# High and low part of a 256-token tile as one 512-column matmul operand, in a two-block fp32 network on one Trainium2 core

## The chip, the cores and the metric

One core of a Trainium2 chip runs the whole program. The time is device microseconds of one execution. The engines are TensorE (PE in the profile, its weight loads PEld), VectorE (DVE), ScalarE (ACT), GpSimd (POOL) and SyncE (SP), which issues the DMAs.

## The reference, cut to what matters

A batch of one, 256 tokens, width 1024, all in float32. A first block of two layers, then a second block of two layers in which a second stream (ctx, also 256 tokens) goes along. Every layer is made of feed-forwards and mixers between residuals; nearly all of the work is `activation @ weight`.

```
# first block, each of two layers
x = x + 0.5 * swiglu_ffn(rms_norm(x, g1), w_in, w_out)     # 1024 -> 2 x 2816 -> 1024
rx, rgate, q, k, v, f, ga, gb = split(rms_norm(x, g2) @ w_in)
ya = (rg_lru(causal_dwconv(rx)) * gelu(rgate)) @ w_rnn_out
yb = forgetting_attention(q, k, v, f) @ w_attn_out         # 8 heads of 128, q and k normed per head
x = x + (sigmoid(ga) * ya + sigmoid(gb) * yb) @ w_o
x = x + 0.5 * swiglu_ffn(rms_norm(x, g3), ...)
x = x + sigmoid(rms_norm(x, g4) @ w_gate + b) * (p @ w_proj)
# second block: layer 0 has a convolution module, layer 1 windowed attention with context keys
x   = x   + 0.5 * gt1 * swiglu(modulate(x, ...));   ctx = ctx + 0.5 * cg1 * swiglu(modulate(ctx, ...))
x   = x   + gt2 * (conv or attention of x);         ctx = ctx + cg2 * conv of ctx      # layer 0
x   = x   + 0.5 * gt3 * swiglu(modulate(x, ...));   ctx likewise in layer 0
return rmsnorm(x, final_g)
```

## The kernel before, in words

Activations stand feature-major: 128 features on the partitions, 256 tokens (or both streams, 512) in the free dimension, so a linear layer takes a [128, 128] weight tile as the stationary operand and moves 256 token columns past it. To keep float32 accuracy with the faster float32r matmul, every weight and every activation is split in two parts, high and low, and `mm3` (lines 293 to 297) adds three products in PSUM: high weight by high activation, high by low, low by high.

`Chunk` (lines 271 to 289, called `load`) brings up to sixteen weight tiles by one DMA into `wraw` (two buffers) and splits them in pieces of 1024 columns: ScalarE's cast gives `whi` (line 281), VectorE's subtraction `wlo` (line 282), five buffers of each. The high and low activations lie in separate `big` buffers.

PSUM has eight banks of [128, 512] floats. The pool `pm` has four one-bank buffers with the tag `mm` for the linear layers, `pst` three for small things, `pad` one. `gemm_pair` makes two output tiles side by side in one bank, 16 weight tiles, 48 matmuls. What reads PSUM afterwards is the operation itself: the multiplication with the norm (L420, L652, L663, L719), the residual (`stt`, L370), a Silu (L889), and so on.

First block (`ffn1st`, `mix`, `ple`): only x exists; the norm's factor per token is applied at the eviction, so that matmuls needn't wait for it. `mix` computes q, k and v token-major, with the activation as the stationary side and 256 weight columns moved at a time (`gemm_tok`), norms each head of q and k (squares on ScalarE, L578; powers on GpSimd; scaling on VectorE, L586), and transposes it back on TensorE (L590). Between these, `lru_front` runs the recurrent branch on VectorE and ScalarE.

Second block: `Feed.ins` and `Feed.outs` are a feed-forward, `Conformer` the convolution module, `attend` the attention. `modnorm` makes the split, normed input tile by tile; here the norm comes before the matmul. `pair_s` works on one stream (256 columns), with two chunks at a time where a stage starts, `pair_j` on both (512 columns). Where both streams run together the matmuls have 512 columns already.

`Background` runs the depthwise convolution of the context, a chain of VectorE operations, between the groups of the first block's second layer: each group hands out an estimate of free VectorE time. `filler` runs the modulation's matmuls (L748) in the same manner. The instructions of each engine stand in a fixed order, made when the program is built: the earliest in the program goes first among those that a simulated timeline finds ready.

Of the kernel before, what the change touches and what calls it, by code (L numbers as in the profile page):

```python
# [17 lines left out]
P = 128  # L18
D = 1024
KT = 8  # L20
# [114 lines left out]
def layout(inputs):  # L135
# [35 lines left out]
    for l in range(2):  # L171
# [9 lines left out]
        out[f"qkv{l}"] = _lay_cols(w[:, 2048:5120], 256)  # L181
# [31 lines left out]
def tile_body(ctx, tc, I, out, stop=None, dbg=None):  # L213
# [8 lines left out]
    pm = ctx.enter_context(tc.tile_pool(name="pm", bufs=4, space=PSUM))  # L222
# [75 lines left out]

    def after(ins):
# [3 lines left out]
    def ps(tag="mm"):  # L303
        pool = {"mm": pm, "st": pst, "ad": pad}[tag]
        return pool.tile([P, 512], F32, tag=tag, name=nm("ps" + tag))
# [20 lines left out]
    class Sq:  # L326
        """running sum of squares of one stream's eight feature tiles"""
# [17 lines left out]
    def rs_cols(sq, inv, eps):  # L345
        """[128 tokens, 2] = (inv * column sums + eps) ** -0.5"""
# [13 lines left out]
    def bcast(r):  # L360
        """[128, 256] with r[token] on every partition: in PSUM and copied"""
# [14 lines left out]
    # =====================================================================  # L376
    # first block
    # =====================================================================
    class Pre:
        """gain * x split in two, tile by tile as x is finished, with the sum of squares"""  # L380

        def __init__(self, gain):
            self.gain = gain
            self.h = None

        def add(self, n):
            if self.h is None:
                self.h = bigt([P, KT, S], F32R)
                self.l = bigt([P, KT, S], F32R)
                self.sq = Sq()  # L390
            x = X[:, n, 0:S]
            g = vc(self.gain, n)
            A.activation(self.h[:, n, :], x, AF.Copy, scale=g)
            stt(self.l[:, n, :], x, g, self.h[:, n, :], ALU.mult, ALU.subtract)
            self.sq.add(x)
# [9 lines left out]
    def gemm_pair(W, hh, hl):  # L405
        """two output tiles [128, 256] of a 2048-element chunk, in one bank"""
        b = ps()
        ks = [(j, k) for j in range(2) for k in range(KT - 1)] + [(j, KT - 1) for j in range(2)]
        for j, k in ks:
            mm3(b[:, j * S : (j + 1) * S], *W(j * KT + k), hh[:, k, :], hl[:, k, :], j == 0 and k == 0, j == 1 and k == KT - 1)  # L410
        return b

    def ffn1st(pre, fi, fo, after, hook, first=None):
        pre.done()
        ah = [bigt([P, 8, S], F32R) for _ in range(3)]
        al = [bigt([P, 8, S], F32R) for _ in range(3)]
        for f in range(FT):
            b = gemm_pair(first if first and f == 0 else load(I[fi][f]), pre.h, pre.l)
            t = tmp(512)
            V.tensor_tensor(out=v2(t), in0=v2(b), in1=pre.Rb, op=ALU.mult)  # L420
# [4 lines left out]
            split(ah[f // 8][:, f % 8, :], al[f // 8][:, f % 8, :], a)  # L425
            hook("in", f)
        for n in range(KT):
            b = ps()
            for r in range(2):
                W = load(I[fo][n, :, r * 11 * P : (r + 1) * 11 * P], 11 * P)  # L430
                for j in range(11):
                    f = 11 * r + j
                    mm3(b[:, 0:S], *W(j), ah[f // 8][:, f % 8, :], al[f // 8][:, f % 8, :], f == 0, f == FT - 1)
            x = X[:, n, 0:S]
            stt(x, b[:, 0:S], 0.5, x, ALU.mult, ALU.add)
# [3 lines left out]
    def softplus_table():  # L439
        """2 * softplus(-lam), both layers: [128, 16]"""  # L440
# [23 lines left out]
    def atanh2(o, w, z, h):  # L464
        """o = 2 atanh(w) for 0 <= w <= 1/3 (series to w**15)"""
# [6 lines left out]
    def mix(l, pre, after):  # L472
        pre.done()
        hh, hl, R, Rb, r = pre.h, pre.l, pre.R, pre.Rb, pre.r
        # r2e = eps * (mean(x^2) + eps) per token, for the head norms on unscaled q, k
# [15 lines left out]
        for k in range(KT):  # L491
            mm3(pf[:8, 0:S], fh[:, k * 8 : k * 8 + 8], fl[:, k * 8 : k * 8 + 8], hh[:, k, :], hl[:, k, :], k == 0, k == KT - 1)
# [10 lines left out]
        # minus log sigmoid, then its running sum = -dcum  # L503
# [23 lines left out]
        def lru_front(n):  # L527
            """xb <- -(1 + tanh) x d, th <- tanh(-log a / 2), at <- a, with d = 1 / (1 + th)"""
# [12 lines left out]
            # d from exp, then one Newton step: -d = ((1 + th) d0 - 2) d0  # L541
# [13 lines left out]
        for c in range(4):  # L555
            b = gemm_pair(load(I[f"rx{l}"][c]), hh, hl)
            for j in range(2):
# [825 lines left out]
```

## Time and profile before

| what | us |
|---|---|
| median of three runs | 3210.55 |
| lowest and highest run | 3207.67, 3215.64 |
| span of the profiled execution | 3207.8 |
| VectorE busy in that span | 1939.8 |
| ScalarE busy in that span | 1468.9 |

The profile lists no time of the profiled execution but its span, from the first to the last instruction; it lies within 0.1% of the median. In the profile a matmul's duration is modelled and includes its way through the array: neighbours overlap, so that the price of a matmul in a stream is the distance from one start to the next. Durations on VectorE overlap a little in the same way.

### The profile page before, as it was taken

What the parts mean: (1) busy time and instruction counts of PE and PEld (TensorE: products, weight loads), DVE (VectorE), ACT (ScalarE), POOL (GpSimd) and SP (SyncE); (2) the same over time, 40 slices, a digit from 0 to 9 for tenths busy, and PEclk for the clock granted to TensorE, in tenths of its full rate; (3) what the DMA queues carried; (4) which work ended last, traced back from release to release, by engine and by line L of the source; (5) the groups of instructions that cost most, each with busy time, mean ns of one, the idle gap of its engine ahead of it and who ended that gap; (6) DMA issues with size and microseconds to landing.
All of it is one profiled execution on the core that took longest, in us unless ns stands there. A gap on an engine that the chain in (4) does not pass through costs nothing.

```text
span 3207.8 us, 55462 instructions
## 1 busy us (share of the span) xinstructions
PE 3138.7 (98%) x23080; PEld 2916.9 (91%) x23080; DVE 1939.8 (60%) x3139; ACT 1468.9 (46%) x2421; POOL 341.5 (11%) x410
## 2 busy tenths in 40 slices
PE   9999999999999999999999999999999999999998
PEld 8899899999999999899999998878888888895898
DVE  6557666556558998668767557954333433356554
ACT  4446654445445446545555446643222322246443
POOL 1010102011010010001011025410002000110101
PEclk9999999999999999999999999989999999999999
DMA  7664346764454554345554554775222223230354
GB/s 284 266 231 164 127 163 238 272 221 167 172 183 171 177 188 166 129 160 188 178 175 159 173 169 168 279 285 188 92 87 97 98 88 110 77 112 34 132 177 139
DMA packets 84252, 536.02 MB, mean 167 GB/s; under 512 B 10016, under 2 KB 13088, under 8 KB 32416
## 3 DMA queue, kind: packets, MB, share of 16 engines
q1 hardware_dynamic: 84000, 532.48, 46.9%
q8 instruction: 180, 2.95, 0.4%
q14 instruction: 72, 0.59, 0.0%
HBM read 531.39 MB, written 1.05 MB: 166 GB/s over the span
## 4 chain that ended last, share of the span: by engine, by line
PE 92%; DVE 3%; ACT 1%; POOL 1%; issue 1%; DMA 1%; POOLq 0%; DVEq 0%; SPq 0%; ACTq 0%
PE psmm L294 28%; PE psmm L295 28%; PE psmm L296 28%; PE psad L748 2%; DVE wlo L282 1%; DVE big L370 1%; PE psad L1133 1%; PE psst L1125 1%; PE psst L350 1%; POOL tmp L342 1%; ACT whi L281 1%; DVE tmp L370 1%; PE psst L296 0%; PE psst L294 0%; PE psst L295 0%
## 5 line engine op out<-in xcount | busy, mean ns | idle before, releaser
L294 PE MATMUL psmm<-big,whi 128*128 128x256 f32 (+1 forms) x6546 | 1955.3, 300 | 14.8 <-ACT big L841 10.9
L295 PE MATMUL psmm<-big,whi 128*128 128x256 f32 (+1 forms) x6546 | 1955.6, 299 | 5.0 <-DVE big L370 5.0
L296 PE MATMUL psmm<-big,wlo 128*128 128x256 f32 (+1 forms) x6546 | 1952.6, 299 | 3.1 <-DVE wlo L282 3.1
L281 ACT CAST whi<-wraw 128x1024 fp32r<-128x1024 f32 (+2 forms) x940 | 904.6, 973 | 1320.4 <-PE psmm L295 941.8
L282 DVE TENSOR_TENSOR wlo<-wraw,whi 128x1024 fp32r<-128x1024 f32 (+2 forms) x940 | 1067.2, 1144 | 689.1 <-ACT whi L281 677.9
L294 PEld LDWEIGHTS psmm<-big,whi 128*128 128x128 f32 x6546 | 1260.6, 193 | 88.4 <-issue 19.8
L295 PEld LDWEIGHTS psmm<-big,whi 128*128 128x128 f32 x6546 | 1262.5, 193 | 46.7 <-issue 7.1
L296 PEld LDWEIGHTS psmm<-big,wlo 128*128 128x128 f32 x6546 | 1261.7, 193 | 44.4 <-issue 5.5
L335 POOL TENSOR_TENSOR tmp<-X 128x256 f32<-128x256 f32 x20 | 15.7, 792 | 1670.5 <-DVE X L370 1620.1
L370 DVE SCALAR_TENSOR_TENSOR big<-U,vec,big 128x256 f32<-128x256 f32 x392 | 188.9, 496 | 4.0 <-ACT big L977 0.5
L890 DVE TENSOR_TENSOR tmp<-tmp,psmm 128x256 f32<-128x256 f32 (+1 forms) x120 | 58.9, 491 | 122.8 <-PE psmm L296 118.7
L373 ACT CAST big<-tmp 128x256 fp32r<-128x256 f32 (+1 forms) x210 | 92.5, 441 | 82.8 <-DVE tmp L424 65.1
L420 DVE TENSOR_TENSOR tmp<-psmm,tmp 128x512 f32<-128x512 f32 x88 | 60.7, 690 | 106.3 <-PE psmm L296 105.5
L296 PE MATMUL psmm<-whi,big 128*128 128x256 f32 x416 | 118.3, 284 | 2.0 <-DVE big L370 2.0
L341 POOL TENSOR_TENSOR tmp<-X 128x256 f32<-128x256 f32 x100 | 83.9, 848 | 329.6 <-DVE X L370 272.5
L294 PE MATMUL psmm<-whi,big 128*128 128x256 f32 x416 | 118.8, 286 | 0.1
L295 PE MATMUL psmm<-wlo,big 128*128 128x256 f32 x416 | 118.1, 284 | 0.0
L374 DVE TENSOR_TENSOR big<-tmp,big 128x256 fp32r<-128x256 f32 (+1 forms) x210 | 97.7, 467 | 20.0 <-ACT big L373 19.4
L342 POOL TENSOR_TENSOR tmp<-tmp,tmp 128x256 f32<-128x256 f32 x100 | 102.6, 1030 | 5.3
L370 DVE SCALAR_TENSOR_TENSOR X<-psmm,mods,X 128x256 f32<-128x256 f32 x96 | 43.5, 480 | 74.7 <-PE psmm L296 72.9
L296 PEld LDWEIGHTS psmm<-whi,big 128*128 128x128 f32 x416 | 79.7, 192 | 2.4 <-DVE big L370 2.2
L295 PEld LDWEIGHTS psmm<-wlo,big 128*128 128x128 f32 x416 | 79.8, 192 | 0.1
(271 smaller groups left out, 2012.1 us busy)
## 6 DMA issues: line engine op xcount, KB each, us to landing
big<-ada SPq DMA_DIRECT2D x72, 1024.0 KB, 9.6
wraw<-fi_c SPq DMA_DIRECT2D x66, 1024.0 KB, 4.9
wraw<-fi_d SPq DMA_DIRECT2D x52, 1024.0 KB, 4.9
wraw<-fi_b SPq DMA_DIRECT2D x44, 1024.0 KB, 4.9
wraw<-fi_a SPq DMA_DIRECT2D x43, 1024.0 KB, 4.9
wraw<-fo_c SPq DMA_DIRECT2D x48, 704.0 KB, 4.0
wraw<-qkv SPq DMA_DIRECT2D x24, 1024.0 KB, 4.9
wraw<-pw SPq DMA_DIRECT2D x24, 1024.0 KB, 4.9
```

Source lines behind the costliest of these rows:

```text
L281: A.copy(hi[:, :e], raw[:, o : o + e])
L282: V.tensor_sub(lo[:, :e], raw[:, o : o + e], hi[:, :e])
L294: T.matmul(o, wh, xh, start=start, stop=False)
L295: T.matmul(o, wh, xl, start=False, stop=False)
L296: newest[1] = T.matmul(o, wl, xh, start=False, stop=stop).ins
L341: G.tensor_tensor(out=q, in0=src, in1=src, op=ALU.mult)
L342: G.tensor_tensor(out=self.acc, in0=self.acc, in1=q, op=ALU.add)
L370: V.scalar_tensor_tensor(o, a, s, b, op0, op1)
L373: A.copy(hi, src)
L374: V.tensor_sub(lo, src, hi)
L420: V.tensor_tensor(out=v2(t), in0=v2(b), in1=pre.Rb, op=ALU.mult)
L748: T.matmul(p_[32 * q : 32 * q + 32, :], cs[:, 4 * h + q, 16 - 2 * b : 48 - 2 * b], raw[:, q * 512 : (q + 1) * 512], start=b == 0 and h == ...
```

## The change

The high and low part of an activation tile now lie next to each other in one buffer, `Split`, as [128, tiles, 2, 256]. `mm2` moves both halves past the high weight tile in one matmul of 512 columns, which fill one whole PSUM bank, and then the high half past the low weight tile in one of 256 columns. The sum of the bank's two halves is made when it is read: `add2` copies one half by ScalarE and adds the other by VectorE, into a buffer of its own; `residual` adds the two halves to X one after the other. Two output tiles need two banks, so `pm` becomes two buffers of two banks. `gemm_tok` moves 512 weight columns at a time in place of 256. Where both streams already give 512 columns, in `pp` of `ple`, in `keys_values`, and in the last chunk of the queries, `mm3` stays.

```diff
-    pm = ctx.enter_context(tc.tile_pool(name="pm", bufs=4, space=PSUM))
+    pm = ctx.enter_context(tc.tile_pool(name="pm", bufs=2, space=PSUM))
+    def mm2(o, wh, wl, x, start, stop):
+        T.matmul(o, wh, x, start=start, stop=False)
+        newest[1] = T.matmul(o[:, 0], wl, x[:, 0], start=False, stop=stop).ins
+        return newest[1]
+    class Split:
+        def __init__(self, nt, w=S):
+            self.per = 1024 // w
+            self.t = [bigt([P, self.per, 2, w], F32R) for _ in range(-(-nt // self.per))]
+        def __call__(self, n, c=slice(None)):
+            return self.t[n // self.per][:, n % self.per, :, c]
+    def banks():
+        return pm.tile([P, 2, 512], F32, tag="mm", name=nm("psmm"))
+    def halves(b):
+        return b.rearrange("p a (h s) -> p a h s", h=2)
+    def add2(b):
+        t, u = tmp(512), tmp(512)
+        A.copy(v2(t), halves(b)[:, :, 1])
+        V.tensor_tensor(out=v2(u), in0=halves(b)[:, :, 0], in1=v2(t), op=ALU.add)
+        return u
+    def residual(x, b, j, scale):
+        for h in range(2):
+            stt(x, halves(b)[:, j, h], scale, x, ALU.mult, ALU.add)
...
-    def gemm_pair(W, hh, hl):
-        b = ps()
+    def gemm_pair(W, x):
+        b = banks()
...
-            mm3(b[:, j * S : (j + 1) * S], *W(j * KT + k), hh[:, k, :], hl[:, k, :], j == 0 and k == 0, j == 1 and k == KT - 1)
+            mm2(halves(b)[:, j], *W(j * KT + k), x(k), k == 0, k == KT - 1)
+    def scaled(b, Rb):
+        u = add2(b)
+        V.tensor_tensor(out=v2(u), in0=v2(u), in1=Rb, op=ALU.mult)
+        return u
...
-            t = tmp(512)
-            V.tensor_tensor(out=v2(t), in0=v2(b), in1=pre.Rb, op=ALU.mult)
+            t = scaled(b, pre.Rb)
...
-            stt(x, b[:, 0:S], 0.5, x, ALU.mult, ALU.add)
+            residual(X[:, n, 0:S], b, 0, 0.5)
...
-        def gemm_tok(W):
-            b = ps()
+        def gemm_tok(c):
+            b = banks()
+            Ws = [load(I[f"qkv{l}"][c, h]) for h in range(2)]
+            for k in range(KT):
+                for m in range(2):
+                    tok = slice(m * P, (m + 1) * P)
+                    w = Ws[k // 4](k % 4, 512)
+                    T.matmul(b[:, m], px.h(k, tok), w[0], start=k == 0, stop=False)
+                    T.matmul(b[:, m], px.h(k, tok), w[1], start=False, stop=False)
+                    T.matmul(b[:, m], px.l(k, tok), w[0], start=False, stop=k == KT - 1)
+            return b
...
-    def pair_s(Ws, H, s, tag="mm"):
-        bs = [ps(tag) for _ in Ws]
+    def pair_s(Ws, H, s):
+        bs = [banks() for _ in Ws]
...
-            mm3(bs[i][:, j * S : (j + 1) * S], *Ws[i](j * KT + k), H.h(k, col(s)), H.l(k, col(s)), k == 0 and j == 0, k == KT - 1 and j == 1)
+            mm2(halves(bs[i])[:, j], *Ws[i](j * KT + k), H(k, col(s)), k == 0, k == KT - 1)
...
-                            use(f + q, col(s), b[:, 0:S], b[:, S:512])
+                            t = add2(b)
+                            use(f + q, col(s), t[:, 0:S], t[:, S:512])
```

## Rows read from the trace of the kernel before

**Rows 1.** The page: span, busy time by engine, chain that ended last by engine.
```profile
span 3207.8 us, 55462 instructions
...
PE 3138.7 (98%) x23080; PEld 2916.9 (91%) x23080; DVE 1939.8 (60%) x3139; ACT 1468.9 (46%) x2421; POOL 341.5 (11%) x410
...
PE 92%; DVE 3%; ACT 1%; POOL 1%; issue 1%; DMA 1%; POOLq 0%; DVEq 0%; SPq 0%; ACTq 0%
```

**Rows 2.** PE's groups by shape: xcount | busy us, mean ns | idle before.
```profile
L295 PE MATMUL psmm<-big,whi 128*128 128x256 f32 x5700 | 1626.1, 286 | 5.0 <-DVE big L370 5.0
...
L295 PE MATMUL psmm<-big,whi 128*128 128x512 f32 x846 | 329.5, 390 | 0.0
...
L294 PE MATMUL psmm<-whi,big 128*128 128x256 f32 x416 | 118.8, 286 | 0.1
```

**Rows 3.** PE's timeline, 256 columns: start, us, instruction; 45 matmuls apart.
```profile
101.26 0.28 PE L296 MATMUL psmm<-big,wlo 128*128 128x256 f32 x1
...
106.65 0.28 PE L296 MATMUL psmm<-big,wlo 128*128 128x256 f32 x1
```

**Rows 4.** PE's timeline, 512 columns, 14 matmuls apart.
```profile
2299.69 0.39 PE L294 MATMUL psmm<-big,whi 128*128 128x512 f32 x1
...
2302.86 0.39 PE L296 MATMUL psmm<-big,wlo 128*128 128x512 f32 x1
```

**Rows 5.** Windows: stretch, us, busy PE PEld DVE ACT POOL (x), PEclk, DMA, GB/s.
```profile
490.00:510.00 20.00, 18.89 (x159) 18.69 (x158) 18.96 (x24) 12.12 (x18) 12.95 (x12) 1.00 0.49 163
...
955.00:1111.00 156.00, 153.73 (x1270) 153.64 (x1270) 141.24 (x253) 84.36 (x119) 2.01 (x7) 0.99 0.50 172
1111.00:1186.00 75.00, 75.00 (x628) 75.00 (x627) 66.19 (x114) 33.79 (x50) 12.51 (x20) 1.00 0.61 204
...
1213.00:1301.00 88.00, 84.18 (x675) 82.53 (x674) 70.96 (x148) 64.68 (x156) 8.40 (x7) 1.00 0.42 145
...
1460.00:1536.00 76.00, 76.00 (x636) 76.00 (x635) 61.54 (x98) 42.03 (x56) 1.54 (x4) 1.00 0.53 187
...
2000.00:2100.00 100.00, 97.68 (x789) 85.17 (x788) 84.84 (x161) 61.51 (x124) 39.83 (x57) 0.98 0.72 282
...
3006.00:3130.00 124.00, 124.00 (x1020) 124.00 (x1019) 66.25 (x89) 57.78 (x86) 0.00 (x0) 0.98 0.50 171
```

**Rows 6.** VectorE's groups by shape, columns as in rows 2.
```profile
L282 DVE TENSOR_TENSOR wlo<-wraw,whi 128x1024 fp32r<-128x1024 f32 x804 | 988.6, 1238 | 540.7 <-ACT whi L281 529.8 <-PE psmm L295 3.0 <-PE psst L364 2.1
...
L420 DVE TENSOR_TENSOR tmp<-psmm,tmp 128x512 f32<-128x512 f32 x88 | 60.7, 690 | 106.3 <-PE psmm L296 105.5 <-ACT tmp L366 0.5
...
L370 DVE SCALAR_TENSOR_TENSOR X<-psmm,X 128x256 f32<-128x256 f32 x48 | 19.4, 418 | 15.7 <-PE psmm L296 15.1
```

**Rows 7.** ScalarE's groups by shape.
```profile
L281 ACT CAST whi<-wraw 128x1024 fp32r<-128x1024 f32 x804 | 833.8, 1048 | 1076.8 <-PE psmm L295 698.4 <-issue 133.7 <-PE psmm L296 41.1
...
L1126 ACT COPY big<-psst 128x512 f32<-128x512 f32 x32 | 18.1, 594 | 16.7 <-PE psst L1125 16.6
```

**Rows 8.** VectorE's timeline beside the background: [idle before <-releaser].
```profile
1052.28 0.69 DVE L420 TENSOR_TENSOR tmp<-psmm,tmp 128x512 f32<-128x512 f32 x1 [0.81 <-PE psmm L296]
...
1058.04 0.69 DVE L420 TENSOR_TENSOR tmp<-psmm,tmp 128x512 f32<-128x512 f32 x1 [0.95 <-PE psmm L296]
1058.64 0.48 DVE L370 SCALAR_TENSOR_TENSOR big<-U,vec,big 128x256 f32<-128x256 f32 x1
```

**Rows 9.** VectorE's timeline at 107 us, and where the context's first feed-forward starts.
```profile
106.97 0.69 DVE L420 TENSOR_TENSOR tmp<-psmm,tmp 128x512 f32<-128x512 f32 x1 [2.18 <-PE psmm L296]
...
768.27 2.36 DVE L282 TENSOR_TENSOR wlo<-wraw,whi 128x1024 fp32r<-128x1024 f32 x2 [4.16 <-ACT whi L281]
770.55 0.41 DVE L890 TENSOR_TENSOR tmp<-tmp,psmm 128x256 f32<-128x256 f32 x1
```

**Rows 10.** PE's waits: who <- for whom: us in total, times, longest us.
```profile
PE psmm L294 <- ACT big L841: 10.9, 4, 4.2
...
PE psst L590 <- DVE tmp L586: 8.9, 6, 2.7
```

More of the change, by code (lines that the diff above doesn't have):

```diff
@@ L432, in ffn1st @@
                     f = 11 * r + j
-                    mm3(b[:, 0:S], *W(j), ah[f // 8][:, f % 8, :], al[f // 8][:, f % 8, :], f == 0, f == FT - 1)
-            x = X[:, n, 0:S]
-            stt(x, b[:, 0:S], 0.5, x, ALU.mult, ALU.add)
+                    mm2(halves(b)[:, 0], *W(j), ax(f), f == 0, f == FT - 1)
+            residual(X[:, n, 0:S], b, 0, 0.5)
             after.add(n)
@@ L555, in mix @@
         for c in range(4):
-            b = gemm_pair(load(I[f"rx{l}"][c]), hh, hl)
-            for j in range(2):
-                V.tensor_tensor(out=rx[:, 2 * c + j, :], in0=b[:, j * S : (j + 1) * S], in1=R, op=ALU.mult)
+            b = gemm_pair(load(I[f"rx{l}"][c]), px)
+            V.tensor_tensor(out=rx[:, 2 * c : 2 * c + 2, :], in0=v2(add2(b)), in1=Rb, op=ALU.mult)
         qT = bigt([P, KT, S])
@@ L571, in gemm_tok @@
             return b
         def qk(c, dst, gain):
-            b = gemm_tok(load(I[f"qkv{l}"][c]))
-            ss = sm(4)
-            for j in range(4):
+            b = gemm_tok(c)
+            ss = sm(8)
+            for j in range(8):
                 jk = tmp()[:, :P]
-                A.activation(jk, b[:, j * P : (j + 1) * P], AF.Square, accum_out=ss[:, j : j + 1])
-            v = sm(4)
+                A.activation(jk, b[:, j // 4, (j % 4) * P : (j % 4 + 1) * P], AF.Square, accum_out=ss[:, j : j + 1])
@@ L591, in qk @@
-            h0 = 2 * (c % 4)
-            o = dst[:, h0 : h0 + 2, :].rearrange("p a b -> p (a b)")
-            A.activation(o, pt, AF.Copy, scale=gain)
+                V.tensor_scalar(v[:, 4 * m : 4 * m + 4], ss[:, 4 * m : 4 * m + 4], 1.0 / P, em[:, m : m + 1], ALU.mult, ALU.add)
+            f = sm(8)
+            G.tensor_tensor(out=f, in0=v, in1=mhalf[:, 0:8], op=ALU.pow)
+            ys = []
+            for m in range(2):
+                y = tmp(512)
+                ys.append(y)
+                for j in range(4):
+                    V.tensor_scalar(y[:, j * P : (j + 1) * P], b[:, m, j * P : (j + 1) * P], f[:, 4 * m + j : 4 * m + j + 1], None, ALU.mult)
@@ L595, in mix @@
+            for e in range(2):
+                pt = ps("st")
+                for m in range(2):
+                    for hd in range(2):
+                        T.transpose(pt[:, hd * S + m * P : hd * S + (m + 1) * P], ys[m][:, (2 * e + hd) * P : (2 * e + hd + 1) * P], ident)
+                h0 = 4 * (c % 2) + 2 * e
+                o = dst[:, h0 : h0 + 2, :].rearrange("p a b -> p (a b)")
+                A.activation(o, pt, AF.Copy, scale=gain)
         qg = sp.tile([P, 1], F32, tag="qg", name=nm("qg"), bufs=1)
@@ L596, in mix @@
         V.tensor_scalar(qg, vc(f"q_norm{l}"), 1.0 / math.sqrt(128.0), None, ALU.mult)
-        for c in range(8, 12):
-            b = gemm_tok(load(I[f"qkv{l}"][c]))
+        for c in range(4, 6):
+            b = gemm_tok(c)
             for m in range(2):
-                A.activation(vt[:, m, (c - 8) * S : (c - 7) * S], b[:, m * S : (m + 1) * S], AF.Copy, scale=rk[:, m : m + 1])
-            lru_front(c - 8)
-        for c in range(4, 8):
+                A.activation(vt[:, m, (c - 4) * 512 : (c - 3) * 512], b[:, m], AF.Copy, scale=rk[:, m : m + 1])
+            lru_front(2 * c - 8)
+            lru_front(2 * c - 7)
@@ L603, in mix @@
+        for c in range(2, 4):
             qk(c, kT, vc(f"k_norm{l}"))
-            lru_front(c)
-        for c in range(4):
+            lru_front(2 * c)
+            lru_front(2 * c + 1)
+        for c in range(2):
             qk(c, qT, qg)
@@ L955, in head @@
                 with after(marks.get(n - 2)):
-                    b = pair_s([load(I["pw1"][n])], H, s)[0]
+                    b = add2(pair_s([load(I["pw1"][n])], H, s)[0])
                 t = tmp()
@@ L1047, in keys_values @@
                 for k in range(KT):
-                    mm3(b[:, m * S : (m + 1) * S], H.h(k, tb), H.l(k, tb), *Wv(k, S), k == 0, k == KT - 1)
+                    mm3(b[:, m * S : (m + 1) * S], H.h(k, tb), H.l(k, tb), *Wv(k, S), m == 0 and k == 0, m == 1 and k == KT - 1)
             A.copy(vt[:, 2 * h : 2 * h + 2, :].rearrange("p a b -> p (a b)"), b)
-            return pair_s([Wk], H, h)[0]
+            return add2(pair_s([Wk], H, h)[0])
         b = keys_values(1)
@@ L1081, in queries @@
         def queries(c):
-            b = pair_s([load(I["aq"][c])], H, 0, "st" if c == 3 else "mm")[0]
+            W = load(I["aq"][c])
+            if c < 3:
+                b = add2(pair_s([W], H, 0)[0])
+            else:
+                b = ps()
+                for j in range(2):
+                    for k in range(KT):
+                        mm3(b[:, j * S : (j + 1) * S], *W(j * KT + k), H.h(k, xs), H.l(k, xs), j == 0 and k == 0, j == 1 and k == KT - 1)
             q = tmp(512)
```

156 lines of the change are left out of this document (71 added, 85 removed).

## The prediction, made before the changed kernel was built

> **What bounds the kernel now.** I read the page's busy shares and chain first: TensorE is busy for 98% of the span and carries 92% of the chain that ended last; VectorE is busy 60%, ScalarE 46% [rows 1]. A busy share says little of pipelined matmuls, so next I read the spacing. In a dense stretch a 256-column matmul starts every (106.65 - 101.26)/45 = 0.1198 us, a 512-column one every (2302.86 - 2299.69)/14 = 0.2264 us [rows 3, 4]. Twice the columns cost 1.89 times as much, so about 13 ns go with each matmul and not with its columns. The groups by shape tell how many there are: 5700 of each of the three lines of `mm3` with 256 columns, 846 with 512, and 416 where the activation is the stationary side [rows 2]. Last I read the windows by stage: where PE is filled from end to end (3006 to 3130), fewer matmuls are worth their full price; where VectorE is nearly full as well (955 to 1111: 141.2 of 156 us) they are not [rows 5].
>
> **What it saves on TensorE.** `mm2` replaces three 256-column matmuls on a weight tile by one of 512 and one of 256. The columns stay, one matmul and one weight load go. Of the 5700 tiles, 32 in `ple` (its `pp` weights) keep `mm3`, leaving 5668. Per tile: 3 x 0.1198 - (0.2264 + 0.1198) = 0.0132 us; x 5668 = 74.8 us. In `gemm_tok` 384 of the 416 trios become 192 trios of 512 columns (the other 32 are `keys_values`): 576 x (2 x 0.1198 - 0.2264) = 7.6 us. Together 82 us, if all of it lay on the path. No row shows 512 and 256 alternating; I take each form's own price. At best the 256-column one falls to the bare 0.1066 us (the difference of the two spacings), another 75 us, but the 512-column stream has slack beside its loads and still pays its fixed part, so I give this nothing.
>
> The Trainium skill (TensorE: Matmul & The Clock Gate, Back-to-back issue gap) speaks against the change: an isolated warm matmul costs N/2.4 + 2.5 ns, which is 109 and 216 ns, so that a tile would save 2.5 ns and the whole change about 15 us. The trace disagrees: 119.8 and 226.4 ns [rows 3, 4].
>
> **What it adds.** `add2` (259 calls: 144 behind `gemm_pair`, 86 in `Feed.ins`, 16 + 8 in the convolution modules, 5 in `attend`) puts one ScalarE copy and one VectorE add of 128x512 between PSUM and whatever read PSUM before. The nearest rows: copy from PSUM 0.594 us [rows 7], VectorE 512-wide with one PSUM operand 0.690 us [rows 6]. Back to back, VectorE instructions overlap: after such an instruction the next starts 0.60 us later (1058.04 to 1058.64) [rows 8], so I count 0.61. That is 259 x 0.61 = 158 us VectorE and 259 x 0.59 = 153 us ScalarE. `residual` doubles the 256-wide update of X 88 times (feed-forward outputs 64, `wo` 16, `ao` 8): 0.418 us each, 0.40 in the stream [rows 6] = 35 us. VectorE goes to 1940 + 193 = 2133 of about 3180 us (67%), ScalarE to 51%. In the plain feed-forward stages both stay hidden: 3006 to 3130 has VectorE at 66 of 124 us, and its 22 `add2` add 13 [rows 5]. What isn't hidden, part by part:
>
> *VectorE-full stretches.* 955 to 1111: 27 groups (22 of the feed-forward, 5 of the context's pointwise, of 16 tiles) add 16.5 us to 141.2: 157.7 of work, while PE would need 156 - 27 x 16 x 0.0132 = 150.3. VectorE becomes the bound: 158 to 163, where the full saving gives 150; I take 9 us given back. 1111 to 1186: 66.2 + 8 x 0.40 + 2 x 0.61 = 70.6 against 75 - 2.7: just fits. The background's tail after 1460, `rx`, `wo` (18.96 of 20 us before, plus 8 x 0.40 each layer): 4 us. 2000 to 2100: 84.8 + 12 x 0.61 = 92 of 97.5: 4 us.
>
> *q, k, v.* 1213 to 1301 has PE at 84 of 88 us, with VectorE 71 and ScalarE 65 [rows 5], and PE waits 8.9 us on the head norm's VectorE scaling (L590 <- L586) [rows 10]. Both engines' work per head stays, but a chunk is now twice as long, so the chain behind the last one (8 squares, then scales) doubles. Of 7.6 us I keep 3: 4.5 given back (bounds 0 and 15).
>
> *PSUM slots.* `pm` goes from four one-bank slots to two of two banks. A group of 16 tiles takes 5.55 us, and an eviction starts 0.04 us after the last matmul's end (106.93 to 106.97) [rows 9]; copy and add take 1.4 us with their hand-overs, 4.7 behind one cast of 1.05 us and two weight splits of 1.14 [rows 6, 7]. That is under 5.55: hidden. But `pair_s` with two chunks takes both slots at once, and the next group waits for the first `add2`. It happens 8 times: ctx and x of the first Feed, x's part of the second, twice in `c1`, once in `d1`, in both `pw2` starts. Alone the copy and add would cost 1.43 - 0.7 (the last two tiles run after the first chunk's) = 0.8 us; but at 768.27 VectorE runs two splits, 2.36 us, right where the eviction comes, and the eviction starts at 770.55 [rows 9]. Bounds 0.8 and 3; I take 2: 16 us.
>
> *Ends of stages.* Where the next stage waits for the last update, the chain grows by one 0.4 us update or by 1.3 us of `add2`. PE stands still there already (10.9 us in 4 waits for `modnorm`'s first tile, L841) [rows 10]. Five updates and five `add2` in the second block: 8.5 us; the first block applies its norm at the eviction, so little: 1. Bounds 4 and 15. *Heads and attention:* two more t512 buffers per group beside the heads' own, with `bufs` still 4, and scores that free two banks at once: bounds -1 and 10, I take 5, for most groups there end long before their buffer is wanted.
>
> The moved operand now needs both halves, but `mm3`'s second matmul wanted the low half 0.12 us later anyway: nothing. Weights come in the same bytes and pieces; the `qkv` chunks are two loads of the same size: nothing on the queue.
>
> **The sum** against the profiled execution (span 3207.8 us; the median of the runs is 2.7 above it): -82 + 9 + 4 + 4 + 4.5 + 16 + 9.5 + 5 = -30, a span near 3178. On the median of the runs that is 3210.5 - 30 = 3180 us, 0.9% faster.
>
> **Rivals.** (a) *Little is given back*: VectorE runs without a gap in the stretch from 955, each slot wait costs its 0.8 us, the stage ends their lower 4, the rest nothing: -82 + 7.5 + 6.5 + 4 = -64, 3146. For it: in the plain stages VectorE stands idle until PE is done, 2.18 us at 106.97 [rows 9]. Against: the stretches at 955 and 2000. (b) *It cancels*: every serial cost at its upper end: slots 24, q, k, v 15, stage ends 15, heads 10, and VectorE's stretches 13 + 5: 82, so 3210, no change. For it: each of these chains is really there; against: each upper end needs the chain to meet no idle time of PE at all, and PE already stands still at several of these places. (c) *Slower*: with two slots a late eviction stops PE. From 955 to 1186, 1460 to 1536 and 2000 to 2100 run some 407/5.75 = 70 groups beside a VectorE above 80% [rows 5]. Once an `add2` ends more than 5.55 us after its group, each further wait is PE's; the chain above reaches 4.7 without background work, so three background updates of 0.4 us ahead of it decide. At 0.8 us a group: +57 on the forecast, 3237. Against: even at 1052 and 1058 VectorE waited 0.8 to 0.95 us for PE before it evicted [rows 8], so its queue is not late yet. (d) *The 13 ns stay*: if a 256-column matmul behind a 512-column one took 0.133 us, nothing is saved and all costs remain: 3262. Against: the fixed part is the same in both pure streams [rows 3, 4]. The Trainium skill's rule above would leave 15 us of saving and end near 3247.
>
> **How the numbers follow.** Forecast 0.60 (its own range 3155 to 3200), (a) 0.13, (b) 0.12, (c) 0.12, (d) 0.03. The range 3135 to 3225 takes in most of (a), (b), and the mild part of (c). A measurement of this kernel tells about 0.3%, some 10 us, from no change: faster is the forecast and (a), 0.73; same is (b), 0.12; slower is (c) and (d), 0.15.
>
> **What would show it.** In the changed profile: PE instructions down by 5668 + 576 = 6244, to about 16800; spacing of the alternating pair 0.346 us; 3006 to 3130 shortened by 22 x 16 x 0.0132 = 4.6 us, apart from its 2 us slot wait. VectorE's share near 67% and above 96% in the stretch that begins at 955, which should not get shorter. New PE waits on VectorE's add behind each two-chunk `pair_s`, 1 to 3 us. Wrong would be: a pair at 0.36 us (d); many PE waits of 0.3 us and more on the add inside the feed-forwards (c); or the stretch from 955 shrinking to 150 us (a).

## The result and the profile after

The changed kernel takes 3286.7 us in the median (3283.2 to 3291.5), against 3210.0 for the kernel before: a ratio of 1.024, with a 95% interval of 1.0226 to 1.0255. It is 77 us slower; 30 us faster was forecast, and the time lies above the range and above every rival's. The profiled execution took 3283.2 us, its span is 3281.5.

The page of the kernel after, as in [rows 1]:

```profile
span 3281.5 us, 43643 instructions
...
PE 3116.5 (95%) x16836; PEld 2588.8 (79%) x16836; DVE 2125.4 (65%) x3462; ACT 1589.5 (48%) x2672; POOL 343.1 (10%) x402
...
PE 85%; DVE 7%; ACT 3%; issue 2%; DMA 2%; POOL 1%; SPq 0%; POOLq 0%; DVEq 0%; ACTq 0%
```

The change did what it says: 6244 matmuls fewer, 16836 left. VectorE's 2125 us and ScalarE's 1590 are close to the forecast's 2133 and 1622 (1469 + 153). Over the whole span no engine is full. Yet TensorE's part of the chain fell from 92% to 85%, and VectorE's rose from 3% to 7%: the loss is waiting, not work.

TensorE's groups by shape (count | busy us, mean ns | idle before and who ended it), which answer to [rows 2]:

```profile
L302 PE MATMUL psmm<-big,whi 128*128 128x512 f32 x5668 | 2032.7, 402 | 59.8 <-DVE big L417 23.9 <-DVE tmp L346 23.4 <-DVE X L417 5.9
L303 PE MATMUL psmm<-big,wlo 128*128 128x256 f32 x5668 | 1600.3, 283 | 5.6 <-DVE wlo L282 5.6
...
L621 PE MATMUL psmm<-whi,big 128*128 128x512 f32 x192 | 76.8, 401 | 0.0
```

The eviction's own instructions, VectorE's and ScalarE's groups, beside [rows 6, 7]: 0.682 and 0.579 us, where the nearest rows had 0.690 and 0.594.

```profile
L346 DVE TENSOR_TENSOR tmp<-psmm,tmp 128x512 f32<-128x512 f32 x259 | 176.7, 682 | 50.1 <-ACT tmp L345 50.1
```

```profile
L345 ACT COPY tmp<-psmm 128x512 f32<-128x512 f32 x259 | 150.0, 579 | 45.5 <-PE psmm L303 45.1 <-DVE big L1151 0.4
```

TensorE's waits (us in total, times, longest), beside [rows 10]:

```profile
PE psst L647 <- DVE tmp L642: 27.6, 8, 9.5
PE psmm L302 <- DVE big L417: 23.9, 10, 3.9
PE psmm L302 <- DVE tmp L346: 23.4, 19, 3.0
PE psst L397 <- ACT tmp L385: 9.7, 8, 2.8
```

L647 <- L642 is the head norm of q and k (L590 <- L586 before), 8.9 us before and 27.6 now. L397 <- L385 are the norm's column sums, which wait for ScalarE's squares. L302 <- big L417 is the first matmul of a stage that waits for `modnorm`, L302 <- tmp L346 a matmul that waits for an `add2`.

Two views of TensorE's timeline show the pair, at two places of the same trace:

```profile
1049.77 0.39 PE L302 MATMUL psmm<-big,whi 128*128 128x512 f32 x1
1050.00 0.28 PE L303 MATMUL psmm<-big,wlo 128*128 128x256 f32 x1
...
1050.81 0.39 PE L302 MATMUL psmm<-big,whi 128*128 128x512 f32 x1
```

```profile
849.81 0.40 PE L302 MATMUL psmm<-big,whi 128*128 128x512 f32 x1
850.05 0.28 PE L303 MATMUL psmm<-big,wlo 128*128 128x256 f32 x1
...
850.87 0.40 PE L302 MATMUL psmm<-big,whi 128*128 128x512 f32 x1
```

Three pairs take 1.04 us in the one, 1.06 in the other: 347 and 353 ns a pair, where the forecast had 346 and three matmuls of 256 had taken 359. Over the whole trace, away from waits and half clock, the mean pair takes 350 ns.

To see where the 74 us between the two spans come from, I took the distance from each TensorE start to the next in both traces and compared it with the usual distance (lower quartile) for its two shapes. The usual distances sum to 87 us less than before. Small excesses, under 60 ns a matmul, come to 33 us, most of it from the 353 ns rhythm: the quartiles of the pair add up to 345 ns, its mean is 350. Distances stretched by a granted clock at half give 22 us more than before (55.6 for 33.2), and waits 105 more (248 for 143). -87 + 33 + 22 + 105 = +73. How the first two divide depends on what is called usual; their sum, -54, hardly does.

Set side by side at the same weight tile, the plain feed-forwards gain 1 to 2 us per 150 tiles. The loss comes in jumps. The largest are layer 0's q, k, v and heads, +20, layer 1's, +22, the convolution modules and what follows them, 1930 to 2197 in the time of before, +13, 2407 to 2577, where `c1` starts, +11, and the stretch from 2781 through the attention, +14.

Windows of the kernel after over the tiles that lay at 959 to 1111, 1111 to 1213, 1213 to 1303, 2000 to 2100 and 3006 to 3130 before [rows 5]:

```profile
972.20:1121.10 148.90, 148.56 (x846) 130.62 (x845) 139.73 (x240) 91.75 (x134) 3.24 (x6) 0.98 0.50 173
1121.10:1226.80 105.70, 100.98 (x573) 87.03 (x572) 100.97 (x186) 46.75 (x68) 15.30 (x21) 0.98 0.54 182
1227.00:1337.80 110.80, 92.83 (x414) 74.78 (x413) 84.50 (x180) 71.04 (x168) 8.99 (x7) 0.92 0.38 131
2038.90:2146.80 107.90, 99.80 (x628) 77.09 (x627) 91.10 (x173) 67.30 (x137) 47.67 (x62) 0.94 0.59 229
3081.10:3204.70 123.60, 120.62 (x682) 105.20 (x681) 78.03 (x108) 68.65 (x106) 0.00 (x0) 0.98 0.49 171
```

The first part of the stretch beside the background, the one I took to be VectorE's, got shorter, 148.9 for 152.6 us. The part behind it, up to q, k, v, grew from 101.7 to 105.7 us; there VectorE is busy for 101.0 us, 96%, and TensorE waits:

```profile
PE psmm L302 <- DVE X L417: 3.8, 2, 2.4
PE psmm L302 <- DVE tmp L346: 1.0, 1, 1.0
```

The first line stands for residual updates that still hold a slot, the second for a sum that does. The q, k, v stretch grew by 21 us at the same work, and its granted clock fell from 1.00 to 0.92.

### The profile page after: what moved, and what is told of

Its sections match the earlier page's. It is cut to its first block, busy times and chain, and to the rows that moved or that the text cites. A ratio compares the mean times of both kernels' runs of the same rounds, so it can differ in the third digit from the quotient of the medians.

```text
span 3281.5 us, 43643 instructions
## 1 busy us (share of the span) xinstructions
PE 3116.5 (95%) x16836; PEld 2588.8 (79%) x16836; DVE 2125.4 (65%) x3462; ACT 1589.5 (48%) x2672; POOL 343.1 (10%) x402
## 4 chain that ended last, share of the span: by engine, by line
PE 85%; DVE 7%; ACT 3%; issue 2%; DMA 2%; POOL 1%; SPq 0%; POOLq 0%; DVEq 0%; ACTq 0%
PE psmm L302 38%; PE psmm L303 19%; PE psmm L294 6%; PE psmm L295 6%; PE psmm L296 6%; DVE wlo L282 2%; PE psad L798 2%; DVE big L417 2%; ACT whi L281 1%; DVE tmp L417 1%; PE psmm L621 1%; PE psmm L622 1%; PE psmm L623 1%; DVE X L417 1%; PE psad L1195 1%
## 5 line engine op out<-in xcount | busy, mean ns | idle before, releaser
L302 PE MATMUL psmm<-big,whi 128*128 128x512 f32 x5668 | 2032.7, 402 | 59.8 <-DVE big L417 23.9
L303 PE MATMUL psmm<-big,wlo 128*128 128x256 f32 x5668 | 1600.3, 283 | 5.6 <-DVE wlo L282 5.6
L302 PEld LDWEIGHTS psmm<-big,whi 128*128 128x128 f32 x5668 | 1076.5, 190 | 357.5 <-issue 56.0
L303 PEld LDWEIGHTS psmm<-big,wlo 128*128 128x128 f32 x5668 | 1082.7, 191 | 17.1 <-issue 8.0
L294 PE MATMUL psmm<-big,whi 128*128 128x512 f32 (+1 forms) x878 | 340.6, 388 | 5.4 <-DVE tmp L346 3.0
L295 PE MATMUL psmm<-big,whi 128*128 128x512 f32 (+1 forms) x878 | 339.7, 387 | 0.8 <-DVE big L421 0.8
L296 PE MATMUL psmm<-big,wlo 128*128 128x512 f32 (+1 forms) x878 | 339.5, 387 | 0.0
L346 DVE TENSOR_TENSOR tmp<-psmm,tmp 128x512 f32<-128x512 f32 x259 | 176.7, 682 | 50.1 <-ACT tmp L345 50.1
L294 PEld LDWEIGHTS psmm<-big,whi 128*128 128x128 f32 x878 | 166.0, 189 | 42.0 <-issue 4.1
L295 PEld LDWEIGHTS psmm<-big,whi 128*128 128x128 f32 x878 | 166.2, 189 | 33.9 <-DVE big L421 1.1
L296 PEld LDWEIGHTS psmm<-big,wlo 128*128 128x128 f32 x878 | 166.1, 189 | 33.9 <-issue 0.8
L417 DVE SCALAR_TENSOR_TENSOR big<-U,vec,big 128x256 f32<-128x256 f32 x392 | 188.4, 495 | 3.6 <-ACT big L1031 1.2
L345 ACT COPY tmp<-psmm 128x512 f32<-128x512 f32 x259 | 150.0, 579 | 45.5 <-PE psmm L303 45.1
L417 DVE SCALAR_TENSOR_TENSOR X<-psmm,mods,X 128x256 f32<-128x256 f32 x136 | 62.7, 481 | 87.6 <-PE psmm L296 51.5
L462 DVE TENSOR_TENSOR tmp<-tmp,tmp 128x512 f32<-128x512 f32 x120 | 83.1, 692 | 5.5 <-ACT tmp L413 4.4
```

The costliest lines, as they stand in the source:

```text
L294: T.matmul(o, wh, xh, start=start, stop=False)
L295: T.matmul(o, wh, xl, start=False, stop=False)
L296: newest[1] = T.matmul(o, wl, xh, start=False, stop=stop).ins
L302: T.matmul(o, wh, x, start=start, stop=False)
L303: newest[1] = T.matmul(o[:, 0], wl, x[:, 0], start=False, stop=stop).ins
L345: A.copy(v2(t), halves(b)[:, :, 1])
```

## The experiments

The kernel before took 3209 to 3211 us beside each of these runs. Runs 5 to 10 are one execution each; the two to four executions of a kernel lie up to 9 us apart, so that a difference of a few us between single ones says little without the trace. The first question was whether the loss belongs to one part (the wide q, k, v chunks, the two-chunk starts) or to what all parts share (two slots, a longer eviction).

**1. q, k, v as before, in the kernel after.**

```diff
-            b = banks()
-            Ws = [load(I[f"qkv{l}"][c, h]) for h in range(2)]
+            b = banks()[:, 0]                 # 256 weight columns, one chunk
```

> The changed kernel, with q, k and v of the first block computed as before: 256 weight columns per matmul, one bank of a double slot per chunk, head norm by four heads' squares. Theory W (the stream gained what its matmul prices say, and PE now stands where it waits for the end of a longer chain): PE's wait for the head norm's scaling, 27.6 us in the changed kernel, falls to about 10, the two stretches of q, k, v give back 35 of the 39 us they lost, and 7 us of the matmul saving go: 3287 - 28 = about 3259 or, with the half clock that follows long waits, 3250. Rival S (it is two PSUM slots in place of four): a narrow chunk holds a double slot for half the time, but only two are in flight in place of four, the head norm's wait stays near 25 us and the time goes up by the lost saving: 3287 to 3295.

3288.8 us: no change, as rival S had it, with some 7 us of the saving given up. The waits for the head norm even grew, to 34.4 us in 9, and layer 1's q, k, v took 116.8 us where the kernel after has 111.0. The width of the chunks isn't what costs.

**2. Two-chunk starts in one slot, in the kernel after**, with three matmuls and no `add2` there.

```diff
-        bs = [banks() for _ in Ws]
+        b2 = banks(); bs = [b2[:, 0], b2[:, 1]]      # for two chunks, mm3
```

> The changed kernel, but where a stage of the second block starts with two chunks side by side, both go into the two banks of one slot, with three matmuls of 256 columns and no add after it. Theory W: the waits of PE for the add of a two-chunk start (23.4 + 3.0 + part of 2.0 us in the changed kernel) fall under 5, 16 chunk passes lose 16 x 16 x 0.013 = 3 us of saving: 3287 - 25 = 3262, and a few us less half clock. Rival: those waits only cover others (the low part of the normed input, L417, 23.9 us); then PE's waits move there and the time stays within 8 us of 3287.

3271.8 us, 15 less, and W's number for it was 3262. The waits for `add2` (L302 <- L346) fell from 23.4 to 12.7 us, those for `modnorm` from 23.9 to 11.4, and one on ScalarE's part of it (L294 <- L887) rose from 2.9 to 10.3. So the forecast's 16 us for these starts was about right, and most of the loss is elsewhere.

**3. The slots alone, in the kernel before:** two slots of two banks; the matmuls and the short evictions stay.

```diff
-pm = ... tc.tile_pool(name="pm", bufs=4, space=PSUM)       # [P, 512]
+pm = ... tc.tile_pool(name="pm", bufs=2, space=PSUM)       # [P, 2, 512]
```

> The kernel before with its three 256-column matmuls and its short evictions, but with two PSUM slots of two banks instead of four of one; a group still fills one bank. This is the slot part of the change alone. Rival S: it costs a large part of the 153 us that lie between the matmul saving and the result, 40 us or more: 3250 and above, spread over the feed-forwards. Theory W: short evictions (0.4 to 0.8 us) leave a slot in time everywhere but at two-chunk starts (8 x 0.7) and in q, k, v, whose head norm holds a slot long (15 to 30 us in both layers): 3230 to 3245, and the plain feed-forwards unchanged.

3260.2 us: +49. Its waits:

```profile
PE psst L595 <- DVE tmp L591: 21.1, 6, 6.0
PE psmm L294 <- DVE U L375: 12.7, 3, 8.5
PE psmm L294 <- DVE tmp L896: 12.6, 5, 3.1
PE psmm L294 <- ACT tmp L1033: 9.7, 3, 9.1
```

The third line is the eviction of the two-chunk starts in `Feed.ins`, the place that I had priced: 12.6 us. The others I had not. U is the convolution module's own eviction of a pointwise chunk, L1033 the eviction of its second pointwise product, and L595 <- L591 the head norm, 12.2 us above before. TensorE and VectorE at the longest of them:

```profile
1988.72 0.71 PE L369 MATMUL psst<-ident,rctx 128*128 128x128 f32 x4 [0.52 <-DVE rctx L1306]
1997.93 0.58 PE L294 MATMUL psmm<-big,whi 128*128 128x256 f32 x1 [8.50 <-DVE U L375]
```

```profile
1995.82 0.48 DVE L375 SCALAR_TENSOR_TENSOR big<-U,vec,big 128x256 f32<-128x256 f32 x1
1996.22 0.48 DVE L375 SCALAR_TENSOR_TENSOR big<-tmp,mods,big 128x256 fp32r<-128x256 f32 x1
1996.61 0.87 DVE L375 SCALAR_TENSOR_TENSOR tmp<-X,mods,tmp 128x256 f32<-128x256 f32 x2
1997.40 0.48 DVE L375 SCALAR_TENSOR_TENSOR U<-psmm,vec,tmp 128x256 f32<-128x256 f32 x1
```

A pointwise chunk stays in its slot until VectorE, busy with convolution taps and `modnorm`, comes to it at 1997.40. With four slots that held one of four. With two, the next feed-forward can't start, and TensorE stands 8.5 us. In the plain feed-forwards the two slots cost 0.0 us per 150 tiles. The size is rival S's, the places are theory W's.

**4. The eviction work alone, in the kernel before:** four slots and three matmuls stay; each place that has an `add2` gets a copy and a second VectorE operation (a maximum of the bank and its copy, which changes nothing), and each `residual` a second update, times zero.

```diff
+    def add2(b):
+        t, u = tmp(512), tmp(512)
+        A.copy(t, b)
+        V.tensor_tensor(out=u, in0=b, in1=t, op=ALU.max)
+        return u
```

> The kernel before with four slots and its three 256-column matmuls, but with the change's eviction work: a 512-wide copy by ScalarE and a 512-wide VectorE operation (a maximum of the bank and its copy, which is the bank again) before each of the 259 reads, and a second update of X that adds nothing, 88 times. Rival E (VectorE and ScalarE work is the price): 40 us or more: 3250 and above, of it 15 to 20 us in the stretch beside the background. Theory W: longer chains at the ends of stages, 10 to 20 us, and 8 us beside the background: 3228 to 3240.

3273.6 us: +63, rival E's size. Again 0.0 in the plain feed-forwards, and 0.0 beside the background, where E had 15 to 20. Its waits:

```profile
PE psst L599 <- DVE tmp L595: 20.4, 6, 12.8
PE psst L360 <- ACT tmp L348: 11.3, 7, 3.2
...
PE psst L374 <- DVE sm L808: 5.8, 1, 5.8
...
PE psmm L1117 <- DVE big L1105: 4.9, 1, 4.9
```

The longest, 12.8 us, lies in layer 1's q, k, v. The others are ends of chains: the norm's squares (L348) and factors (L808), and the attention's queries (L1105).

**5. Both at once, without the pairs.** Do the two costs add, or are they the same waits counted twice?

```diff
 # the edits of 3 and of 4 together, matmuls as before
```

> The kernel before with both side works of the change at once, and without its matmuls: two slots of two PSUM banks in place of four of one, and the change's eviction work (a copy and a second VectorE instruction on each pair of output tiles, every residual update done twice, the second time with the bank times zero). The three matmuls of 256 columns stay. Alone the slots had cost 49 us and the eviction work 63. Theory P (each costs at its own places, the costs add): 3320 to 3325 us, and nothing in the plain feed-forwards. Rival I (both make the same waits, and the later of two counts): 3275 to 3295. Rival J (they work on each other: with two slots every late eviction stops TensorE): above 3340. The kernel after less this run is what the pairs of 512 and 256 columns give by themselves: under P about -35, under I about 0.

3324.0 us: +115, where 49 + 63 = 112. In the total they add. What the pairs and the wide q, k, v give by themselves is then 3286.7 - 3324.0 = -37 us, not -82.

**6. The kernel after without the sum of the halves.**

```diff
-            u = add2(b)
-            V.tensor_tensor(out=v2(u), in0=v2(u), in1=Rb, op=ALU.mult)
+            V.tensor_tensor(out=v2(u), in0=halves(b)[:, :, 0], in1=Rb, op=ALU.mult)
```

> The kernel after without the sum of the two halves: every eviction reads the first half alone, with the instructions of the kernel before, and each residual update is done once. Left out of the computation: the product of the high part of the weights with the low part of the activations is computed in PSUM and never added. Theory P: the eviction work goes, and its 63 us with it, 3220 to 3230 us. Rival I (slots and eviction make the same waits): the slots keep most of them, 3250 to 3270. Rival C (what was lost is in the matmul pairs themselves, by their uneven spacing and a slower clock): 3270 or more.

3213.0 us, even less than theory P's 3220 to 3230: the eviction costs 74 us in the kernel after, 63 in the kernel before. Against run 3, which has the same slots and evictions, the pairs and the wide q, k, v give 3260.2 - 3213.0 = 47 us here.

**7. The order of the matmuls of two tiles, in the kernel after.**

```diff
         T.matmul(o, wh, x, start=start, stop=False)
+        if not held and not stop:
+            held.append((o[:, 0], wl, x[:, 0], stop))
+            return
+        for p, w, y, e in held + [(o[:, 0], wl, x[:, 0], stop)]:
+            T.matmul(p, w, y, start=False, stop=e)
```

> The kernel after with the matmuls of two weight tiles in the order 512, 512, 256, 256 columns in place of 512, 256, 512, 256; same instructions, same work. In the kernel after a pair takes 347 ns in some stretches and 353 in others, some 22 us in all above the shortest spacings. Theory: the turn from a long to a short matmul at each weight tile costs the extra, and half as many turns save half of it: two tiles 692 to 700 ns, 3270 to 3280 us. Rival: the spacing belongs to the stream of columns and weight loads whatever the order, 3284 to 3290. Rival: with two short matmuls behind one another a weight load is no longer hidden, over 700 ns per two tiles and above 3295.

3285.1 us: no change. The timeline of TensorE:

```profile
1050.02 0.62 PE L302 MATMUL psmm<-big,whi 128*128 128x512 f32 x2
1050.48 0.40 PE L308 MATMUL psmm<-big,wlo 128*128 128x256 f32 x2
1050.71 0.63 PE L302 MATMUL psmm<-big,whi 128*128 128x512 f32 x2
1051.18 0.39 PE L308 MATMUL psmm<-big,wlo 128*128 128x256 f32 x2
1051.41 0.40 PE L302 MATMUL psmm<-big,whi 128*128 128x512 f32 x1
```

Four tiles take 1.39 us; over the whole trace the median of two tiles is 696 to 698 ns in nearly every 50 us. The two rhythms are gone. A tile takes 348.5 ns, 2 less than the mean pair of the kernel after: the spacing that the theory asked for, worth some 10 us of stream. The time shows nothing of it. In this one execution layer 1's q, k, v took 117.0 us for 111.0 at the same tiles, and distances at half clock and waits together some 15 us more, so run 7 decides about the spacing and not about its price. The third rival falls: two tiles stay under 700 ns.

**8 and 9. The background's debt.** In the kernel after little was lost beside the background up to 1121 us, in run 4 nothing, and in both much behind it. The background is the context's convolution. Its last step on VectorE in the kernel before, after, and in run 4:

```profile
1203.63 0.47 DVE L370 SCALAR_TENSOR_TENSOR big<-U,vec,big 128x256 f32<-128x256 f32 x1
```

```profile
1256.98 0.47 DVE L417 SCALAR_TENSOR_TENSOR big<-U,vec,big 128x256 f32<-128x256 f32 x1
```

```profile
1269.26 0.47 DVE L380 SCALAR_TENSOR_TENSOR big<-U,vec,big 128x256 f32<-128x256 f32 x1
```

It had ended 9 us ahead of q, k, v, and now runs into them. If that is a cause, a shorter convolution must help the kernel after and not the kernel before.

```diff
-                    stt(c, u[:, j : j + S], w(j), c, ALU.mult, ALU.add)
+                    if npe or j < 17:
+                        stt(c, u[:, j : j + S], w(j), c, ALU.mult, ALU.add)
```

> The kernel before with less work in the background: of the 30 multiply-adds for each of the eight tiles of the context's convolution on VectorE 14 are left out (112 instructions of 0.42 us, 47 us of VectorE; the output lacks those taps). The control for the run beside it. Theory D (a debt: VectorE's backlog of the background stretch comes due behind it, in layer 1's q, k, v): in the kernel before the convolution is done at 1204 us, ahead of q, k, v, so little waits for it, 3200 to 3210 us. Rival V (VectorE bounds the background stretch itself in both kernels): the stretch from 955 to 1151 gets shorter by 5 us or more, below 3203.

> The kernel after with the same 112 multiply-adds of the context's convolution left out. In the kernel after that convolution ends at 1257 us, in the midst of layer 1's q, k, v, where TensorE then stands 9.5 us; in the kernel before it ends at 1204. Theory D (the added VectorE work of the evictions isn't paid in the background stretch but delays the background, and what is left of it stops q, k, v): the convolution ends before 1215, the waits in layer 1's q, k, v shrink, and 10 to 20 us more than in the kernel before are saved: 3262 to 3278 us. Rival Q (q, k, v wait for their own chunks, whatever the background does): 3280 to 3290.

Before 3209.3 us, unchanged; after 3275.2, 11.5 us less. In the short version the convolution ends at 1188 us in both, and the waits for the head norm between 1190 and 1330 us are, first in the kernel after, then in the shortened one:

```profile
PE psst L647 <- DVE tmp L642: 16.7, 4, 9.5
```

```profile
PE psst L647 <- DVE tmp L642: 12.5, 4, 4.4
```

The total lies within theory D's range, but the gain isn't where the theory has it. The stretch ahead of q, k, v and q, k, v themselves, over the same tiles as 1121.1 to 1226.8 and 1226.8 to 1337.8 in the kernel after:

```profile
1114.70:1213.00 98.30, 98.30 (x573) 85.92 (x572) 80.31 (x134) 45.82 (x65) 12.09 (x18) 1.00 0.58 200
1213.00:1322.80 109.80, 96.02 (x416) 77.20 (x415) 79.08 (x166) 70.85 (x168) 8.04 (x4) 0.91 0.37 130
```

Ahead of q, k, v 7.4 us are regained, 98.3 for 105.7, and TensorE is filled from end to end. In q, k, v it is 1.2 us, 109.8 for 111.0: the wait of 9.5 us became 4.1, but others there grew, one to 4.4. 12.5 us of waiting for the head norm stay, against 4.6 in the kernel before. Run 6, with two slots, no sums, and its convolution done at 1196 us, waits there too: 14.7 us, the longest 9.3. So the debt is real and worth 7 us, it is paid where VectorE works it off, and it isn't what stops q, k, v in the kernel after. The rest of the 11.5 us (8.1 between the two profiled spans) can't be laid to the background: 5.6 us of it lie ahead of the convolution's first step, where the edit takes nothing away, and 7 are lost again behind q, k, v. In the kernel before the stretch ahead of q, k, v takes 101.7 us with the 112 steps and without them: VectorE doesn't bound it there, and in the kernel after it does.

**10. The doubled updates alone, in the kernel before.**

```diff
+    def residual(x, b, scale):
+        stt(x, b, scale, x, ALU.mult, ALU.add)
+        stt(x, b, 0.0, x, ALU.mult, ALU.add)
```

> The kernel before with every residual update of a 256-column output tile done twice (the second time with the bank times zero), and none of the change's other eviction work. It splits the 63 us of the eviction in two. Theory E (each added instruction costs where TensorE waits for the end of a chain, the last tile of a stage; 88 updates at 0.45 us, mostly under way beside matmuls): 12 to 20 us, 3222 to 3230. Rival (the copies and sums alone cost): 3209 to 3214. Rival (the updates cost most, as they stand ahead of the norm's squares): 3245 or more.

3225.1 us: +16. So of the 63 us some 16 are the 88 second updates (35 us of VectorE), and, if the two add, 47 the copies and sums.

**11 and 12. The pairs only where nothing is given back.** Four one-bank slots and `mm3` everywhere except in the feed-forwards of one stream, without their first and last inner tile and their last output tile: 3270 of 5668 tiles. The last run has them in the order of run 7.

```diff
+            if 0 < f < FT - 1:
+                t = gemm_two(W, pre.x)      # two one-bank tiles, mm2, each half copied and added
+            else:
+                b = gemm_pair(W, pre.h, pre.l)
```

> The kernel before (four slots of one bank, three matmuls) with the pair of 512 and 256 columns only where neither slots nor eviction cost anything in the runs so far: in the seven feed-forwards of one stream, without the first and the last of the inner tiles and without the last output tile, 3270 of 5668 weight tiles; two banks a group there, each half copied and added on its own. By the rows: 3270 tiles at 7 to 13 ns each, 23 to 43 us. Theory P (the cost of the change sits at stage starts and in the serial places, not in the plain feed-forwards): 3167 to 3190 us. Rival I (two banks a group and the longer eviction give it back at the turns of the stages, 2 to 4 us at each of 14): 3200 to 3225. Rival C (the pairs lose by the clock): above 3225.

> The version with pairs in the feed-forwards of one stream alone (3187 us), with the matmuls of two weight tiles in the order 512, 512, 256, 256. Two tiles took a steady 696 to 697 ns in that order in the kernel after, 348.5 a tile, against 347 or 353 in the order 512, 256. In the 3187 us version most stretches run at 353. Theory: 3270 tiles at 2 to 4 ns, 6 to 12 us less, 3175 to 3181. Rival: nothing is left of it, since VectorE and the weight casts give the pace there, 3184 to 3190.

3187.1 us (ratio 0.9929, 0.9913 to 0.9946) and 3182.4 us (0.9921, 0.9905 to 0.9938): both faster than the kernel before by less than 1%, with intervals clear of 1; the second by 26 us, 8.1 ns for each tile. The 4.7 us between them, with ranges that touch (3184.5 to 3187.8 and 3181.3 to 3186.8), stay open. The page of the second has TensorE back at 98%:

```profile
PE 3105.7 (98%) x19810; PEld 2732.8 (86%) x19810; DVE 2060.8 (65%) x3462; ACT 1540.8 (48%) x2695; POOL 349.6 (11%) x410
```

It adds as many VectorE instructions as the full change, 3462 in all, though narrower ones (121 us of VectorE's time where the full change adds 186), and still comes out ahead. With the 0.0 of runs 3 and 4 in the plain feed-forwards this says that an added eviction's cost is decided by where it stands more than by how many there are.

## Why the prediction was wrong

*The saving.* The count of matmuls and the price of each form were right: 346 ns a pair, and 347 where the pair runs at its shorter rhythm. Taking each form at its own price hid that their alternation has a second rhythm; with it the mean pair is 350 ns, which takes some 24 us back, and by the distances the stream gives -54, not -82. The Trainium skill (TensorE: Matmul & The Clock Gate, Back-to-back issue gap) has N/2.4 + 2.5 ns for an isolated warm matmul, from which an estimate of 109 + 216 = 325 ns a pair follows; the traces, streams with a weight load for each matmul, show 347 and 353. Rival (d), a pair at 0.36 us, was wrong too, though 353 ns is half of the way to it. Of the 54 us only 37 to 47 show in runs 5 and 6. That a shorter stream only waits longer where TensorE waits anyway would explain it; no run shows that by itself.

*PSUM slots: the first step that failed.* I gave them 16 us; alone they cost 49. I asked how long a feed-forward group holds its bank and who takes both slots at once. Both answers were good: hidden in the feed-forwards, and 12.6 us at the two-chunk starts. I didn't ask who else holds a slot, and for how long: a pointwise chunk that waits for VectorE, the second pointwise product, a chunk of q or k that lies in PSUM until its scaling. Those are 12.7, 9.7 and 12.2 us.

*VectorE-full stretches: right in kind and, for the first, in size; wrong in place.* I let VectorE's overload be paid between 955 and 1111 us, 9 us, and said that the 75 us behind would just fit. It came the other way round. The background's operations are nobody's input for a long while, so they slid: the convolution ended 53 us later by the clock, some 40 against TensorE's own progress. The first part lost under 2 us of its saving (3.7 gained of the 5.3 that its 347 ns rhythm promises). The part up to q, k, v, into which the work slid, had VectorE at 96% and lost 7.4 (105.7 us, 98.3 in run 9 and in run 6). That the two make 9 is luck. The row that I cited against rival (c), VectorE waiting 0.8 to 0.95 us for TensorE before an eviction [rows 8], showed how: evictions go ahead of the background there. I read it as room.

*q, k, v.* Forecast 4.5 us with an upper bound of 15. Both layers lose about 20 (with their heads). My reason, the doubled chunk, wasn't it: run 1 undid it and won nothing. Over the weight tiles of layer 1's q, k, v the traces have 89.8 us in the kernel before, 104.9 with the slots alone, 102.6 with the eviction work alone, 115.9 with both, 111.0 in the kernel after, and 105.1 without its sums. So the slots cost some 15 us there and the eviction some 6 to 13, in whatever width; the convolution's tail only 1.2.

*Ends of stages, heads and attention.* 14.5 us were set for them, 17 for the VectorE stretches and 4.5 for q, k, v: 36 in all, against 63 for the same eviction work by itself, and 16 by the doubled updates alone, for which the 9.5 of the ends held some 3. As I read it, each end was mis-sized in the same way: I counted the added instruction (0.4 or 1.3 us), not the wait that it makes with what is queued before it (up to 12.8 us in run 4). No run prices a single end.

*The clock.* Nothing in the sum stood for it. Most waits of over 2 us have a stretch at half clock in them or right behind them. After the 9.5 us wait in q, k, v the window 1277.15 to 1282 has:

```profile
1277.15:1282.00 4.85, 4.85 (x18) 4.01 (x19) 2.08 (x8) 2.08 (x5) 0.00 (x0) 0.62 0.01 3
```

a mean granted clock of 0.62 between the levels 0.5 (1.2 GHz) and 1.0 (2.4 GHz). In the whole trace this makes some 22 us more than before.

*The rivals.* (c) had the sign, and two slots with late evictions as its cause. Of its places the one from 2000 to 2100 lost 8 us (107.9 for 100.1) and the end of the background stretch 4; but it spread 57 us over 70 groups, and most of the loss lies in q, k, v, at stage starts and in the heads. A sign of (a) came true, the stretch from 955 shrank to 148.9 us, and meant nothing for the whole, since its work had only moved. (b) was the nearest in its reasoning: every serial cost at its upper end. Even those ends, 82 us in all, were short of the 112 to 115 that slots and eviction cost.

What stays open: which state sets the rhythm of 347 or 353 ns (it changes between stretches, and the stretch beside the background had 347 in the kernel after and 353 in run 11), how the 47 us of the copies and sums divide among the heads, the convolution modules and the attention, and whether run 4's 12.8 us wait in q, k, v, beside a convolution that runs until 1269 us, is the background's. Any added instruction also moves others in the order fixed at the build, so that single places can't be priced to better than a few us.

## What to carry to other kernels

Before taking away half of a buffer pool, list every holder of a buffer and how long it holds it; the slow, rare ones decide, not the stream for which the pool was sized. An instruction added to an eviction is free inside a long stream, as long as its engine has room there, and dear in front of each chain that TensorE waits for, so apply such a change group by group: 58% of the tiles gave 26 us where all of them lost 77. When an engine is full, don't ask only who waits there: look at what can slide, and at where it will stand when it is due.

## What the runs showed of the hardware

A 512-column matmul followed by a 256-column one takes 347 ns in some stretches and 353 in others (three pairs in 1.04 or 1.06 us), stable over hundreds of pairs, 350 in the mean, with 226 + 120 expected from the pure streams. In the order 512, 512, 256, 256 one rhythm is left, 697 ns for two tiles.
